# The SBUF pools of a two-layer hybrid decoder are created in another order

## The chip, the cores and the metric

The kernel runs on one core of a Trainium2 chip. The metric is device time in microseconds (us) for one execution. Engines are named as in the profile: PE is the matmul engine (TensorE), PEld its weight loads, DVE the vector engine, ACT the scalar engine, POOL the GpSimd engine, SP the engine that issues most DMAs. L365 is line 365 of the kernel.

## The reference

Two layers act on 256 tokens of width 1024, in float32:

```
h += 0.5 * SwiGLU_1(RMSNorm(h))                       # width 2816
u  = RMSNorm(h);  P = u @ W_in                        # one combined projection
y  = retention, Mamba-2 SSD, latent attention, differential attention   (256 x 512 each)
h += W_out( sum_i sigmoid(gate_i(u)) * (y_i @ W_branch_i) )
h += CrossAttention(RMSNorm(h), RMSNorm(mem))         # 4 heads, 256 memory rows
h += 0.5 * SwiGLU_2(RMSNorm(h))
```

and a last RMSNorm. Almost all of the arithmetic is in products of the 256 tokens with weight matrices.

## The kernel before

**Weights.** They are streamed from HBM in the order of use, in tiles of up to [128, 2048] float32 (1 MB). `fetch` issues one DMA on SP's queue into a tile `wr` (L327), then splits it in two float32r parts whose sum it is: ACT copies it, rounded, into `wh` (L334), and DVE writes the difference into `wl` (L335), each in two halves. There are three buffers each of `wr`, `wh` and `wl`. One tile is made ready ahead of the one that the matmuls use.

**Activations.** They are transposed on PE and split in the same way into high and low parts: `xh`, `xl` for the normed stream (pool `xp`, four tiles of 4 KB in each partition), and 4 KB tiles of pool `mp` (eleven buffers) for everything else: `hid` (the SwiGLU's hidden values), `yr`, `ym`, `yl`, `yd` (the four mixers), `xo0`, `xo1` (cross attention), `mm` (the memory). Smaller work tiles are in `fp` and `sp`, constants and `h` in `cp`.

**Products.** Each is three matmuls of parts: high times high, low times high, high times low. There are two loops that do nearly all of them.

```python
    def linear(kt, n, xT, evacs):          # L351; the matmul is L365
        ...
                for b in range(NB):
                    begin()
                    for part, w in ((0, hi), (1, hi), (0, lo)):
                        for k in range(m):
                            ...
                            pe.matmul(p_[b][:, :n], lhsT=xT(part, k0 + k)[:, b * P:(b + 1) * P],
                                      rhs=w[:, k * n:(k + 1) * n], start=first, stop=last)

    def linear_t(xT, evac):                # L371; the matmul is L383
        ...
                            o = k * 512 + (i * 2 + j) * P
                            pe.matmul(ps[i][:, j * 256:(j + 1) * 256], lhsT=ws[w][:, o:o + P], rhs=xT(part, k0 + k),
```

`lhsT` is the stationary operand (loaded by PEld, 128 columns) and `rhs` the moving one. In `linear` the activations are stationary and 512 columns of weights move; in `linear_t` 128 columns of weights are stationary and the 256 tokens move. PE's instructions keep the order in which they are written; the other engines' order is set by the tile framework, which also adds the waits. Chains of smaller steps (softmax, convolution, transposes) are put between the matmuls by hand.

**Pools.** `program` opens eight SBUF pools (L156 to L163). The framework puts them one behind the other in the order in which they are opened, from byte 16512 of each partition up, and the tiles of a pool likewise. All tiles that L365 and L383 read start at a whole number of 512 bytes from the start of their pool (4096 or 8192 bytes for a tile, 512, 1024 or 2048 for a slice in it); the one exception is the 424-column projection, whose slices are 1696 bytes apart.

Of the kernel before, what the change touches and what calls it, by code (L numbers as in the profile page):

```python
# [16 lines left out]
PSUM = bass.MemoryType.PSUM  # L17
# [13 lines left out]
BUCKETS = 32  # L31
# tiles of weights that are made ready before the matmuls that are traced
AHEAD = 1

# columns of w_in by use
_sizes = (256, 256, 512, 512, 512, 1024, 8, 256, 128, 32, 512, 512, 512, 4096)
_at = np.concatenate([[0], np.cumsum(_sizes)])
(O_RQ, O_RK, O_RV, O_RG, O_Z, O_XBC, O_DT, O_CQ, O_CKV, O_KR, O_DQ, O_DK, O_DV, O_GL) = (int(v) for v in _at[:-1])
# groups of 512 columns, in the order in which they are streamed
G_QK, G_RV, G_RG, G_X0, G_X1, G_Z, G_DQ, G_DK, G_DV, G_GL = range(10)  # L40
_groups = [O_RQ, O_RV, O_RG, O_XBC, O_XBC + 512, O_Z, O_DQ, O_DK, O_DV] + [O_GL + 512 * i for i in range(8)]
MISC = 256 + 128 + 32 + 8

# per-partition parameters of one layer: (name, columns)
_pcols = [("ffn1", 8), ("mix", 8), ("xa", 8), ("mem", 8), ("ffn2", 8), ("ssm", 4), ("qn", 2), ("kvn", 1), ("dn", 1),
          ("cw", 32), ("cb", 8)]
# parameters that every partition needs, of one layer
_bcols = [("dtb", 8), ("alog", 8), ("dsk", 8), ("lam", 256)]
# [11 lines left out]
BO, NBC = _offsets(_bcols)  # L60
# constants that depend on shapes alone
CO, NCC = _offsets([("ident", 128), ("tri", 384), ("dmask", 256), ("inv", 48), ("sel", 8), ("dec", 4 * 256)])
# [37 lines left out]
def lay(x, mem, positions, **w):  # L100
    """The program's inputs: the arrays given, laid out; and constants."""
    a = {k: np.asarray(v) for k, v in w.items()}
# [45 lines left out]
def program(tc, a, out, upto="all"):  # L148
# [4 lines left out]
    def sb(name, bufs):  # L153
        return ctx.enter_context(tc.tile_pool(name=name, bufs=bufs))

    cp = sb("cp", 1)  # L156
    wr = sb("wr", 3)
    wh = sb("wh", 3)
    wl = sb("wl", 3)
    xp = sb("xp", 1)  # L160
    fp = sb("fp", 2)
    sp = sb("sp", 4)
    mp = sb("mp", 11)  # L163
    lin = ctx.enter_context(tc.tile_pool(name="lin", bufs=4, space=PSUM))
# [23 lines left out]

    # ---- inputs that stay
    h = [[cp.tile([P, 512], F32, tag=f"h{b}{c}", name=f"h{b}{c}") for c in range(2)] for b in range(NB)]  # L190
# [31 lines left out]

    # ---- the order of work: linears one after another, and chains of smaller steps between them.
    # A chain yields how many half tiles of weights it lets pass, or what has to have happened before it goes on.
    chains = []
# [37 lines left out]

    # ---- weights, fetched in the order of use
    def chunks(srcs, kt, n):
# [43 lines left out]
    todo = list(plan())  # L309
    # a recent instruction of VectorE, for what is to be spread over the linears  # L310
    paced = None
    fetched = []
    # the last of the instructions that split weights, for what is to be queued behind it
    last = None

    def fetch(first=False):
        """The next tile of weights, as two float32r parts whose sum they are. The first one comes in pieces."""
        nonlocal last
        if not todo:
            return  # L320
        src, n = todo.pop(0)
        r = wr.tile([P, 2048], F32, tag="wr", name="wr")
        hi = wh.tile([P, 2048], F32R, tag="wh", name="wh")
        lo = wl.tile([P, 2048], F32R, tag="wl", name="wl")
        pieces = 4 if first else 2
        if not first:
            nc.sync.dma_start(r[:, :n], src)  # L327
        for i in range(pieces):
            s = slice(i * n // pieces, (i + 1) * n // pieces)
            if first:  # L330
                if i == 2:
                    nc.sync.dma_start(h[1][0], a["x"][1, :, :512])
                nc.sync.dma_start(r[:, s], src[:, s])
            last = act.activation(hi[:, s], r[:, s], AF.Copy)  # L334
            dve.tensor_tensor(lo[:, s], r[:, s], hi[:, s].bitcast(F32), ALU.subtract)  # L335
        fetched.append((hi, lo, n))
# [7 lines left out]

    # ---- building blocks
    def split(hi, lo, src):
        """hi + lo = src, in float32r; src is in SBUF or PSUM."""
        act.activation(hi, src, AF.Copy)
        dve.tensor_tensor(lo, src, hi.bitcast(F32), ALU.subtract)

    def linear(kt, n, xT, evacs):  # L351
        """Rows of tokens times weights [kt * 128, n], one or more; evac(b, psum) takes a block of rows."""
        ps = [[lin.tile([P, 512], F32, tag="lin", name="lin") for _ in range(NB)] for _ in evacs]
# [17 lines left out]
    def linear_t(xT, evac):  # L371
        """Weights [1024, 512] transposed times tokens: evac(i, psum) takes 256 columns as [128, 2, 256]."""
        ps = [lin.tile([P, 512], F32, tag="lin", name="lin") for _ in range(2)]
        for k0 in (0, 4):
            ws = weights(2048)
            for i in range(2):
                begin()
                for j in range(2):
                    for part, w in ((0, 0), (1, 0), (0, 1)):
                        for k in range(4):  # L380
                            o = k * 512 + (i * 2 + j) * P
                            # a start clears the flags of the whole bank: one for both halves
                            pe.matmul(ps[i][:, j * 256:(j + 1) * 256], lhsT=ws[w][:, o:o + P], rhs=xT(part, k0 + k),  # L383
# [6 lines left out]
    def transpose4(src, n=4):  # L390
        """Blocks of 128 columns of src, transposed, in one bank: [128, n, 128]."""
        ps = bank("tr")
# [4 lines left out]
    def split_gain(hi, lo, ps, gain, n=4):  # L397
        """hi + lo = a PSUM tile [128, n, 128] times a gain for each partition and n."""
        t = f2("sgt")[:, :n * P].rearrange("p (k t) -> p k t", k=n)
# [6 lines left out]
    def rstd_of(ss, n, m, name):  # L406
        """(ss / n + eps) ** -0.5 of m columns."""
        t = small("rs" + name, m)
# [9 lines left out]
    class Transposed:  # L418
        """src(b, c): [tokens, 512] for two blocks of columns, transposed and split; with a gain for each column.
        Each half starts as its columns are there."""  # L420

# [41 lines left out]
    def rows_of(r, name):  # L463
        """A value for each token, [P, NB], as rows [P, 256] alike on every partition."""
        ps = bank("rowp")
# [56 lines left out]

    # ---- tables that both layers share
    def tables():
# [19 lines left out]
        for b in range(NB):  # L544
# [18 lines left out]
            yield 2  # L563
        # lambda of the differential attention: -lambda for each layer
        for l in range(L):
# [9 lines left out]
            dve.tensor_scalar(nlam[:, l:l + 1], nlam[:, l:l + 1], li, None, ALU.subtract)  # L575
        # relative bias, times 8, with the causal mask: [queries, head, (block 0, keys 0) (block 1, keys 0 and 1)]
        rel = relt[:, :384]
# [9 lines left out]
        for i, t in enumerate(_thresholds()):  # L587
            yield 3
            # not around the change of stage
            while 60 <= now < 72:  # L590
# [8 lines left out]
    def rope(dst, src, tb, n_heads, hf):  # L599
        """dst = src rotated, [P, heads, 2 * hf]; tb: [cos, sin, -sin] of hf columns each."""  # L600
        s = src.rearrange("p h (e d) -> p h e d", e=2)
# [12 lines left out]
    def attend(b, scores, masks, scale, sbt):  # L614
        """Softmax numerators of a block of queries, in sbt [P, n, 256]; the sums' reciprocals. scores: PSUM for each."""
        n, nk = len(scores), (b + 1) * P
# [10 lines left out]
    def probs_t(pT, b, probs):  # L627
        """Transposed probabilities of a block of queries; pT: keys 0 [P, 4, 256] and keys 1 [P, 4, 128]."""
        for kb in range(b + 1):
# [5 lines left out]
    def mixers(l, xT, nxt):  # L635
# [10 lines left out]

        # -- retention
        qk = [f2("qk") for _ in range(NB)]
# [61 lines left out]

        # -- MLA's low ranks, and Mamba's steps
        dtx = small("dtx", 16).rearrange("p (b h) -> p b h", b=2)
# [23 lines left out]
        def mamba():  # L736
            yield ["misc"]
            x = dtx.rearrange("p b h -> p (b h)")
            e, z1, z2, p_ = (small(n, 16) for n in ("sp0", "sp1", "sp2", "sp3"))
            # softplus(x) = max(x, 0) + 2 artanh(e / (2 + e)) with e = exp(-|x|)  # L740
            dve.scalar_tensor_tensor(e, x, -1.0, x, ALU.mult, ALU.min)
# [24 lines left out]
            dve.tensor_copy(gc, pg[:, :16])  # L766
            # the running sums in two parts, for each block of tokens
            gr = sp.tile([P, NB, 16], F32R, tag="gr", name="gr", bufs=1)
# [3 lines left out]
            yield ["x0", "x1"]  # L772
            # xs on tokens
            xdt, xD = two("xdt"), two("xD")
# [65 lines left out]

        # -- Mamba-2: convolution, on channels
        for j in range(2):
# [19 lines left out]

        # -- gates and merge
        mg = []
# [30 lines left out]

        # -- MLA
        qT, kT, v = heads("mqT"), heads("mkT"), two("mv")
# [68 lines left out]

        # -- differential attention
        def on_rows(dst, name):
# [75 lines left out]

    # ---- memory, normalized, transposed and split
    def memory(l, mem, before):
# [187 lines left out]
```

## Time and profile before

| | |
|---|---|
| median of 3 runs | 1603.26 us (1602.47 to 1603.28) |
| span of the profiled execution | 1601.6 us |
| lies around the span | about 1.7 us (median less span) |
| PE busy | 1587.3 us (99%) |
| DVE busy | 1070.4 us (67%) |
| ACT busy | 825.2 us (52%) |
| mean DMA share, rate | about half, 176 GB/s |

The span runs from the first to the last instruction of one profiled execution. PE's busy time is the union of its matmuls' records, whose ends are modelled, so a busy PE does not say how closely the matmuls follow each other: that is read from the distance between their starts.

### The profile page before, as it was taken

The page shows a single profiled execution, that of the slowest core. Times are in us where ns is not written, and L with a number is a line of the kernel's source. Part 1 is how long each engine was busy: PE and PEld are TensorE (multiplying, and loading weights), DVE is VectorE, ACT ScalarE, POOL GpSimd, SP SyncE. Part 2 cuts the span into 40 slices and gives each one's busy share as a digit, 9 for nine tenths or more (in the row PEclk, how much of TensorE's full clock was granted, in tenths as well). Part 3 has the DMA queues.
Part 4 walks back from the last instruction along what each step waited for, and adds up shares of the span by engine and source line. Part 5 has one row for each costly group of instructions (what it writes and reads, how often), then busy time and mean ns, then how long its engine had stood idle before and what let it go on. Part 6 is the DMA issues. An engine that isn't in the chain of part 4 may idle for free.

```text
span 1601.6 us, 20813 instructions
## 1 busy us (share of the span) xinstructions
PE 1587.3 (99%) x8236; PEld 1349.4 (84%) x8236; DVE 1070.4 (67%) x1698; ACT 825.2 (52%) x1221; POOL 27.0 (2%) x39
## 2 busy tenths in 40 slices
PE   8999999999999999999999999999999999999998
PEld 6888889898888988888888888898988899888886
DVE  6787699998777666554465546697656766565543
ACT  6544446656655545444454444475575554454432
POOL 0000000000000000000000000000000000000000
PEclk9999999999999999999999999999999999999999
DMA  7555554454555544555555556444545554455541
GB/s 288 200 178 187 185 175 159 151 169 147 204 184 169 181 155 162 184 184 175 186 192 185 183 174 207 149 158 152 184 150 206 184 183 163 155 177 180 195 171 66
DMA packets 41713, 281.58 MB, mean 176 GB/s; under 512 B 4624, under 2 KB 5008, under 8 KB 9488
## 3 DMA queue, kind: packets, MB, share of 16 engines
q1 hardware_dynamic: 39600, 275.07, 50.2%
q10 hardware_dynamic: 2016, 5.19, 1.0%
q8 instruction: 64, 1.05, 0.3%
q14 instruction: 33, 0.27, 0.0%
HBM read 279.20 MB, written 1.05 MB: 175 GB/s over the span
## 4 chain that ended last, share of the span: by engine, by line
PE 98%; ACT 0%; DMA 0%; issue 0%; DVE 0%; SPq 0%; POOLq 0%; POOL 0%
PE lin L365 78%; PE lin L383 11%; PE tr L394 2%; PE ht L500 1%; PE xs L1094 1%; PE xo L1140 1%; PE up L905 1%; PE my L821 0%; PE ds L990 0%; DMA h<-x 0%; PE ms L941 0%; PE pt L632 0%; ACT wh L334 0%; PE my L823 0%; PE do L1013 0%
## 5 line engine op out<-in xcount | busy, mean ns | idle before, releaser
L335 DVE TENSOR_TENSOR wl<-wr,wh 128x1024 fp32r<-128x1024 f32 (+2 forms) x534 | 624.9, 1195 | 388.1 <-ACT wh L334 385.6
L334 ACT ACTIVATE wh<-wr 128x1024 fp32r<-128x1024 f32 (+2 forms) x534 | 533.4, 1033 | 518.5 <-PE lin L365 398.7
L365 PE MATMUL lin<-wh,xh 128*128 128x512 f32 (+1 forms) x1216 | 334.0, 396 | 0.2 <-ACT wh L334 0.2
L365 PE MATMUL lin<-wh,xl 128*128 128x512 f32 (+1 forms) x1216 | 325.9, 390 | 0.0
L365 PE MATMUL lin<-wl,xh 128*128 128x512 f32 (+1 forms) x1216 | 325.1, 389 | 0.0
L365 PEld LDWEIGHTS lin<-wh,xl 128*128 128x128 f32 x1216 | 228.8, 188 | 48.1
L365 PEld LDWEIGHTS lin<-wl,xh 128*128 128x128 f32 x1216 | 228.8, 188 | 47.7
L365 PEld LDWEIGHTS lin<-wh,xh 128*128 128x128 f32 x1216 | 222.5, 189 | 43.6 <-ACT wh L334 1.2
L365 PE MATMUL lin<-wh,hid 128*128 128x512 f32 x704 | 180.4, 396 | 0.0
L365 PEld LDWEIGHTS lin<-wh,hid 128*128 128x128 f32 x704 | 131.6, 188 | 31.4
L365 PE MATMUL lin<-wl,hid 128*128 128x512 f32 x352 | 97.7, 395 | 0.0
L365 PEld LDWEIGHTS lin<-wl,hid 128*128 128x128 f32 x352 | 66.1, 188 | 16.0
L510 ACT ACTIVATE sg<-lin,rffn 128x256 f32<-128x256 f32 x88 | 40.9, 464 | 65.2 <-PE lin L365 65.1
L596 DVE SCALAR_TENSOR_TENSOR bias<-relt,d,bias 128x384 f32<-128x384 f32 x124 | 69.8, 612 | 0.8
L383 PE MATMUL lin<-xh,wh 128*128 128x256 f32 x384 | 63.2, 287 | 0.0
L383 PE MATMUL lin<-xh,wl 128*128 128x256 f32 x384 | 61.7, 283 | 0.0
L383 PE MATMUL lin<-xl,wh 128*128 128x256 f32 x384 | 61.7, 283 | 0.0
L511 DVE SCALAR_TENSOR_TENSOR toks<-lin,rffn,sg 128x256 f32<-128x256 f32 x88 | 42.3, 481 | 25.7 <-ACT sg L510 25.7
L383 PEld LDWEIGHTS lin<-xh,wh 128*128 128x128 f32 x384 | 53.1, 191 | 0.3
L383 PEld LDWEIGHTS lin<-xh,wl 128*128 128x128 f32 x384 | 53.0, 192 | 0.0
L383 PEld LDWEIGHTS lin<-xl,wh 128*128 128x128 f32 x384 | 52.9, 191 | 0.0
L416 ACT ACTIVATE junk<-h 128x512 bf16<-128x512 f32 x36 | 22.4, 621 | 31.2 <-DVE h L484 17.2
(385 smaller groups left out, 1536.7 us busy)
## 6 DMA issues: line engine op xcount, KB each, us to landing
wr<-gu SPq DMA_DIRECT2D x87, 1024.0 KB, 5.0
wr<-win SPq DMA_DIRECT2D x68, 1024.0 KB, 5.0
wr<-dn SPq DMA_DIRECT2D x40, 1024.0 KB, 4.8
wr<-wbr SPq DMA_DIRECT2D x16, 1024.0 KB, 4.9
wr<-w_out SPq DMA_DIRECT2D x8, 1024.0 KB, 4.9
wr<-xa_wk SPq DMA_DIRECT2D x8, 1024.0 KB, 5.0
wr<-xa_wq SPq DMA_DIRECT2D x8, 1024.0 KB, 4.9
wr<-xa_wv SPq DMA_DIRECT2D x8, 1024.0 KB, 4.9
```

Of the source, the lines that this page charges most:

```text
L334: last = act.activation(hi[:, s], r[:, s], AF.Copy)
L335: dve.tensor_tensor(lo[:, s], r[:, s], hi[:, s].bitcast(F32), ALU.subtract)
L365: pe.matmul(p_[b][:, :n], lhsT=xT(part, k0 + k)[:, b * P:(b + 1) * P], rhs=w[:, k * n:(k + 1) * n], start=first, stop=last)
L383: pe.matmul(ps[i][:, j * 256:(j + 1) * 256], lhsT=ws[w][:, o:o + P], rhs=xT(part, k0 + k), start=k0 + k + part + w + j == 0, stop=k0 + k = ...
L394: pe.transpose(ps[:, k * P:(k + 1) * P], src[:, k * P:(k + 1) * P], ident)
L416: act.activation(j[:, :src.free_size()], src, AF.Square, accum_out=out_)
L500: pe.transpose(ps[:, k, blk(b)], toks[:, b, k * P:(k + 1) * P], ident)
L510: act.activation(sg, ps[:, :256], AF.Silu, scale=xT.r[:, b:b + 1])
L511: paced = dve.scalar_tensor_tensor(toks[:, b], ps[:, 256:], xT.r[:, b:b + 1], sg, ALU.mult, ALU.mult)
L596: dve.scalar_tensor_tensor(bias[:, hd], ge, d8[:, hd, i + 1:i + 2], bias[:, hd], ALU.mult, ALU.add)
L905: pe.matmul(ps[:, :n], lhsT=lowT[p_][:, k0 + k, blk(b)], rhs=wm[w][:, o + k * n:o + (k + 1) * n], start=i == 0, stop=i == len(seq) - 1)
L1094: pe.matmul(ps[:, j], lhsT=q[part][:, 2 * j + k, blk(b)], rhs=kT[c][w][:, 2 * j + k], start=not part + w + k, stop=w + k == 2)
```

## The change

The eight pools are opened in another order. Names, sizes and numbers of buffers stay, and so does all code behind them; comments were dropped, which moves line numbers by one or so (L365 becomes L366, L383 becomes L384).

```diff
+    xp = sb("xp", 1)
+    mp = sb("mp", 11)
+    fp = sb("fp", 2)
     cp = sb("cp", 1)
+    sp = sb("sp", 4)
     wr = sb("wr", 3)
     wh = sb("wh", 3)
     wl = sb("wl", 3)
-    xp = sb("xp", 1)
-    fp = sb("fp", 2)
-    sp = sb("sp", 4)
-    mp = sb("mp", 11)
```

No instruction moves: on every engine the queue of the changed program has the same instructions, operands by name and waits, row for row (2040 rows of PE, 1240 of DVE, 706 of ACT, 37 of POOL, 61 of SP when like neighbours are put together). What moves are the addresses. The built programs have the pools at these bytes of each partition, and the last two columns are the remainders by 256 (those by 128 are in brackets):

| pool | holds | before | after | start mod 256 before | after |
|---|---|---|---|---|---|
| wr | raw weights | 42976 to 67552 | 155424 to 180000 | 224 (96) | 32 (32) |
| wh | high part of weights | 67552 to 92128 | 180000 to 204576 | 224 (96) | 32 (32) |
| wl | low part of weights | 92128 to 116704 | 204576 to 229152 | 224 (96) | 32 (32) |
| xp | xh, xl | 116704 to 133088 | 16512 to 32896 | 224 (96) | 128 (0) |
| mp | hid, mm, yr ... xo1 | 184096 to 229152 | 32896 to 77952 | 32 (32) | 128 (0) |
| fp | work tiles | 133088 to 173024 | 77952 to 117888 | 224 (96) | 128 (0) |
| cp | h, constants | 16512 to 42976 | 117888 to 144352 | 128 (0) | 128 (0) |

## Rows read from the trace of the kernel before

**Rows 1.** The page: busy time (share of the span), number of instructions.

```profile
PE 1587.3 (99%) x8236; PEld 1349.4 (84%) x8236; DVE 1070.4 (67%) x1698; ACT 825.2 (52%) x1221; POOL 27.0 (2%) x39
...
PEclk9999999999999999999999999999999999999999
```

**Rows 2.** The page: the chain that ended last, by engine and by line.

```profile
PE 98%; ACT 0%; DMA 0%; issue 0%; DVE 0%; SPq 0%; POOLq 0%; POOL 0%
PE lin L365 78%; PE lin L383 11%; PE tr L394 2%; PE ht L500 1%; PE xs L1094 1%; PE xo L1140 1%; PE up L905 1%; PE my L821 0%; PE ds L990 0%; DMA h<-x 0%; PE ms L941 0%; PE pt L632 0%; ACT wh L334 0%; PE my L823 0%; PE do L1013 0%
```

**Rows 3.** Line L365 on PE: count, duration ns min/median/max, first and last start.

```profile
L365 PE MATMUL lin<-wh,xh x1216: 349/389/775, 8.4 to 1530.0; 128*128 128x512 f32 x168, 128*128 128x424 f32 x6
L365 PE MATMUL lin<-wh,xl x1216: 349/389/628, 10.3 to 1530.9; 128*128 128x512 f32 x168, 128*128 128x424 f32 x6
L365 PE MATMUL lin<-wl,xh x1216: 353/389/628, 12.0 to 1531.8; 128*128 128x512 f32 x168, 128*128 128x424 f32 x6
L365 PE MATMUL lin<-wh,hid x704: 392/394/483, 136.8 to 1593.4; 128*128 128x512 f32 x176
L365 PE MATMUL lin<-wl,hid x352: 390/394/403, 138.6 to 1593.8; 128*128 128x512 f32 x176
L365 PE MATMUL lin<-wh,mmh x64: 394/394/478, 559.4 to 1378.4; 128*128 128x512 f32 x64
...
L365 PE MATMUL lin<-wh,yrl x32: 393/394/398, 317.5 to 1119.2; 128*128 128x512 f32 x32
```

**Rows 4.** The same for line L383.

```profile
L383 PE MATMUL lin<-xh,wh x384: 277/283/470, 249.9 to 1349.5; 128*128 128x256 f32 x192
...
L383 PE MATMUL lin<-mmh,wh x128: 276/276/367, 509.5 to 1323.3; 128*128 128x256 f32 x128
```

**Rows 5.** The chain in order of time: start us, us, engine and line, matmuls.

```profile
1281.72 16.34 PE lin L365 x72
...
1305.40 19.05 PE lin L383 x168
...
1324.90 17.27 PE lin L383 x144
...
1538.24 56.01 PE lin L365 x240
```

**Rows 6.** The time line of PE where those pieces begin: start us, us, tiles.

```profile
1281.47 1.17 PE L365 MATMUL lin<-wh,xh 128*128 128x512 f32 x4
...
1305.16 0.71 PE L383 MATMUL lin<-mmh,wh 128*128 128x256 f32 x4
...
1324.66 0.71 PE L383 MATMUL lin<-xh,wh 128*128 128x256 f32 x4
...
1538.00 2.11 PE L365 MATMUL lin<-wh,hid 128*128 128x512 f32 x8
```

**Rows 7.** Whole span, PE, one line each: us, busy (instructions), clock, DMA.

```profile
0.00:1601.60 1601.60, 1282.09 (x5472) 1.00 0.51 176
...
0.00:1601.60 1601.60, 187.48 (x1536) 1.00 0.51 176
```

**Rows 8.** What PE, SP's queue and ACT waited for: us in total, times, longest.

```profile
PE lin L365 <- ACT wh L334: 0.2, 1, 0.2
...
SPq L327 <- DVE wl L335: 1301.1, 238, 14.9
...
ACT wh L334 <- PE lin L365: 398.7, 175, 4.5
```

**Rows 9.** Groups by line and form: the two splits; busy us, mean ns | idle before.

```profile
L335 DVE TENSOR_TENSOR wl<-wr,wh 128x1024 fp32r<-128x1024 f32 x502 | 600.2, 1220 | 368.0 <-ACT wh L334 367.3
L334 ACT ACTIVATE wh<-wr 128x1024 fp32r<-128x1024 f32 x502 | 511.5, 1053 | 484.5 <-PE lin L365 371.0 <-issue 85.3 <-PE lin L383 22.6
```

**Rows 10.** DMA issues: count, KB each, us from issue to landing.

```profile
wr<-gu SPq DMA_DIRECT2D x87, 1024.0 KB, 5.0
```

## The prediction

> **What bounds the kernel now.** I read the page first: PE is busy for 99% of the span, at a granted clock of 0.9 or more in every slice [rows 1]. Next the chain that ended last: 98% of it is PE, 78% the matmuls of `linear` (L365) and 11% those of `linear_t` (L383) [rows 2]. The waits say that this is no hidden wait for data: PE waited for a split weight once, for 0.2 us, while ACT waited 398.7 us for PE to give back `wh` buffers, and SP's queue 1301.1 us for `wr` buffers [rows 8]. So the time is the number of matmuls times the distance between their starts, and only that distance, or a new wait, can change it.
>
> Then I asked how large that distance is, and whether it is the same everywhere. It isn't. In the chain in order of time, 72 matmuls of L365 take 16.34 us, which is 226.9 ns each; 240 others of the same line take 56.01 us, 233.4 ns each [rows 5]. The time line shows what differs: the first piece has `xh` as its stationary operand, the second `hid` [rows 6]. For L383 the 144 matmuls with `xh` moving take 17.27 us, 119.9 ns each, and the 168 with `mm` moving 19.05 us, 113.4 ns each [rows 5, 6]. The durations of all of them repeat this: the median is 389 ns with `xh` or `xl` and 394 with every tile of `mp` on L365 (`yr` and `mm` as well as `hid`), and 283 against 276 on L383 [rows 3, 4]. The instructions of each pair have the same shape and type and the same weights' buffers. What differs is the pool in which the activation lies, so it is the address. That is what this change changes.
>
> **How much of the distance can depend on it.** [...] Each matmul then pays beside its columns 226.9 - 214.0 = 12.9 ns (L365, `xh`), 19.4 ns (L365, `hid`), 12.9 ns (L383, `xh`) or 6.4 ns (L383, `mm`). These are 2, 3, 2 and 1 times the same step, 6.5 ns or about 16 columns.
>
> **The change part by part.** No instruction is added, removed or moved, so the whole of the change is in the addresses. Before, weights and `xp` start at 96 bytes past a multiple of 128, `mp` at 32. After, weights start at 32, and `xp` and `mp` at 0. I take the step as the sum of a part for the moving and a part for the stationary operand. L383 gives the first: an activation that moves from 32 is one step (6.5 ns) cheaper than one that moves from 96. L365 gives the second: a stationary operand at 32 is one step dearer than one at 96. Position 0 is in no row. Its bounds are the two positions that are seen on either side of it, 32 bytes away each; I take the cheaper one for both operands, since a tile that starts at 0 lies in whole stretches of 128 bytes. The terms are:
>
> - L365, weights that move go from 96 to 32: 5472 matmuls [rows 7] x 6.5 ns = 35.6 us less. This is a position that was seen, if for another pool.
> - L365, `mp` tiles that are stationary go from 32 to 0. There are 5472 - 3 x 1216 = 1824 of them [rows 3, 7]; at the price of 96 that is 6.5 ns each, 11.9 us less; at the price of 32 nothing.
> - L365, `xh` and `xl` that are stationary go from 96 to 0: 3648 matmuls; nothing at the price of 96, 23.7 us more at that of 32.
> - L383, `xh` and `xl` that move go from 96 to 0: 1536 matmuls of the line [rows 7] less those of `mm` (three pairs of 128, one of which stands in [rows 4]) leave 1152; 7.5 us less at the price of 32, nothing at that of 96. `mm` (384) stays cheap, or loses 2.5 us.
> - L383, weights that are stationary go from 96 to 32: 1536 [rows 7] x 6.5 = 10.0 us more.
> - The other matmuls (some 10% of the chain, mostly transposes and the attention's small products) I leave at nothing: 1228 instructions at one step each would be 8 us at most, and their signs are mixed.
>
> The sum is -35.6 - 11.9 - 7.5 + 10.0 = -45.0 us. Against the profiled span that is 1601.6 - 45.0 = 1556.6 us; the median of the runs is 1.7 us above the span, so 1558 us.
>
> **What hides the rest, and what is late next.** ACT's and DVE's splits also read and write other addresses, and may take longer or shorter. They cost nothing as long as a tile is split faster than it is used: a full tile feeds 24 matmuls, 5.4 us at 226.9 ns and 5.3 us at 220.4, while ACT needs 2 x 1.053 us and DVE 2 x 1.220 us for it [rows 9]. The DMA lands 5.0 us after its issue [rows 10], with three buffers to fill. With the gain PE asks for weights 3% faster, 181 GB/s in place of 176; if the splits were to take twice as long, DVE's 1070 us would become the bound, and no row hints at that.
>
> [...] The rows show an address effect of 6.5 ns on PE alone [rows 3, 5]. [...]
>
> **The rivals.**
>
> *No gain: position 0 is as dear as the dearer neighbour.* Then `xh` on L365 loses 23.7 us, `mp` wins nothing, `xh` and `mm` on L383 pay for 96: -35.6 + 23.7 + 2.5 + 10.0 = +0.6 us, and the time stays at 1603 or 1604 us. [...] For it: nothing in the rows prices 0. Against it: both operands would have to come out at their dear end. Chance 0.08.
>
> *Slower: the distance between the two operands counts, not each one's position.* The rows fit that just as well. Modulo 256, moving start less stationary start is 224 - 224 = 0 where two steps are paid (both lines), 224 - 32 = 192 for `hid` (three steps), 32 - 224 = 64 for `mm` (one step). After, L365 has 32 - 128 = 160, and L383 has 96. The nearest rows are 192 and 64: every L365 matmul would take the 233.4 ns of `hid`, which costs 3648 x 6.5 = 23.7 us, and `xh` on L383 would win 1152 x 6.5 = 7.5 us: +16.2 us, 1619 us. Drawn on as a line (one column for 4 bytes, half a step for 32) L365 pays another 3.3 ns x 5472 = 18 us and L383 wins 3.3 ns x 1536 = 5 us: +29 us, 1632 us. The place is the next weight load, which PEld reads while the matmul before it streams: if the two reads meet in the same part of the memory, their distance decides. It decides as soon as the distance between starts on L365 with `xh` is above 226.9 ns. Chance 0.25.
>
> *A larger gain.* If position 0 is a step better than either neighbour as stationary operand, L365 comes down to some 214 ns and 5472 x 6.5 = 35.6 us more are won: 1523 us. It needs a matmul with nothing beside its columns, which no row shows. Chance 0.09.
>
> *A smaller gain.* One of the two unknown prices is the dear one for some of the tiles, and 10 to 30 us are left of the 45: 1573 to 1593 us. Chance 0.16.
>
> **How the numbers follow.** The forecast itself (1535 to 1573 us, the sum with a quarter of it either way and a little for the small products) gets 0.42; with the larger gain and the smaller one the kernel is faster with 0.67. A measurement of this kernel tells a change from none at about 0.2%, 3.2 us: that leaves 0.08 for no change and 0.25 for slower. Cases of both signs hold much of the chance, so the range reaches from 1532 us (which leaves out most of the larger gain) to 1628 us (which holds the nearer value of the slower rival and leaves out the drawn-on line).
>
> **What would show it.** The median durations and the distance between starts of the four pairs are the test. Right: L365 near 220 ns for `xh` and for `hid` alike (medians equal, at or below 389 ns less 7), and L383 near 120 ns for both activations. The distance rival would show `xh` rise to the 394 ns of `hid` on L365 while L383 with `xh` falls to 276. Rows of PE that are the same as before to the nanosecond would mean that addresses do not matter. The prediction is also wrong if PE begins to wait for `wh` or `wl` by more than a few us, or if ACT's or DVE's split changes by so much that buffers come late.

## The result, and the profile after

The changed kernel takes 1629.7 us (median of 4 runs, 1629.11 to 1630.43), the kernel before 1602.87 us in the runs beside them: a ratio of 1.0167, 95% interval 1.0154 to 1.0179. It is slower by 27 us, where the forecast was 45 us faster (1558 us), and lies 1.7 us above the upper end of the predicted range (1532 to 1628 us). The slower rival, drawn on as a line, had named 1632 us.

The page of the changed kernel: span, and busy us (share of the span) with the number of instructions.

```profile
span 1627.7 us, 20813 instructions
...
PE 1613.9 (99%) x8236; PEld 1355.5 (83%) x8236; DVE 1070.8 (66%) x1698; ACT 825.5 (51%) x1221; POOL 27.0 (2%) x39
```

The instructions are the same in number. DVE and ACT are busy for as long as in [rows 1], to within 0.4 us, and PE for 26.6 us longer, which is the whole of it: the span grew by 26.1 us.

The two lines on PE, to hold against [rows 3, 4] (count, duration ns min/median/max, first and last start):

```profile
L366 PE MATMUL lin<-wh,xh x1216: 353/397/774, 7.9 to 1555.8; 128*128 128x512 f32 x168, 128*128 128x424 f32 x6
...
L366 PE MATMUL lin<-wh,hid x704: 391/397/481, 139.7 to 1619.4; 128*128 128x512 f32 x176
...
L384 PE MATMUL lin<-xh,wh x384: 277/281/469, 253.9 to 1371.7; 128*128 128x256 f32 x192
...
L384 PE MATMUL lin<-mmh,wh x128: 277/281/364, 517.2 to 1345.4; 128*128 128x256 f32 x128
```

What differed before is now equal. On L366 `xh` and `hid` both have a median of 397 ns, dearer than the dearer of the two before (394); on L384 both activations have 281, between the 276 and the 283 of before.

The chain in order of time gives the distance between starts, for the same four pieces as in [rows 5] (start us, us, matmuls):

```profile
1302.22 16.86 PE lin L366 x72
...
1326.50 20.15 PE lin L384 x168
...
1347.10 17.28 PE lin L384 x144
...
1564.08 56.23 PE lin L366 x240
```

That is 234.2 ns for `xh` (before 226.9), 119.9 for `mm` (before 113.4), 120.0 for `xh` on L384 (before 119.9) and 234.3 for `hid` (before 233.4). Over the whole span, the busy time of each line's matmuls (second figure), against [rows 7]:

```profile
0.00:1627.70 1627.70, 1306.16 (x5472) 1.00 0.51 173
...
0.00:1627.70 1627.70, 189.76 (x1536) 1.00 0.51 173
```

L366 took 24.1 us more and L384 2.3 us more. No wait was added: PE still waits once for `wh`, and the splits wait for PE a little longer than in [rows 8].

```profile
PE lin L366 <- ACT wh L335: 0.2, 1, 0.2
...
ACT wh L335 <- PE lin L366: 412.9, 176, 4.5
```

### The profile page after: what moved, and what is told of

Its sections match the earlier page's. It is cut to its first block, busy times and chain, and to the rows that moved or that the text cites. A ratio compares the mean times of both kernels' runs of the same rounds, so it can differ in the third digit from the quotient of the medians.

```text
span 1627.7 us, 20813 instructions
## 1 busy us (share of the span) xinstructions
PE 1613.9 (99%) x8236; PEld 1355.5 (83%) x8236; DVE 1070.8 (66%) x1698; ACT 825.5 (51%) x1221; POOL 27.0 (2%) x39
## 4 chain that ended last, share of the span: by engine, by line
PE 98%; ACT 0%; issue 0%; DMA 0%; DVE 0%; SPq 0%; POOLq 0%; POOL 0%
PE lin L366 78%; PE lin L384 11%; PE tr L395 2%; PE ht L501 1%; PE xo L1141 1%; PE xs L1095 1%; PE up L906 1%; PE my L822 0%; PE ds L991 0%; PE ms L942 0%; DMA h<-x 0%; PE pt L633 0%; ACT wh L335 0%; PE my L824 0%; PE do L1014 0%
## 5 line engine op out<-in xcount | busy, mean ns | idle before, releaser
L366 PE MATMUL lin<-wh,xh 128*128 128x512 f32 (+1 forms) x1216 | 340.4, 402 | 0.2 <-ACT wh L335 0.2
L366 PE MATMUL lin<-wh,xl 128*128 128x512 f32 (+1 forms) x1216 | 333.7, 396 | 0.0
L366 PE MATMUL lin<-wl,xh 128*128 128x512 f32 (+1 forms) x1216 | 333.3, 396 | 0.0
L366 PEld LDWEIGHTS lin<-wl,xh 128*128 128x128 f32 x1216 | 229.7, 189 | 54.7
L366 PEld LDWEIGHTS lin<-wh,xl 128*128 128x128 f32 x1216 | 229.5, 189 | 54.3
L366 PEld LDWEIGHTS lin<-wh,xh 128*128 128x128 f32 x1216 | 223.1, 189 | 49.3 <-ACT wh L335 1.2
L366 PE MATMUL lin<-wh,hid 128*128 128x512 f32 x704 | 181.1, 397 | 0.0
L366 PEld LDWEIGHTS lin<-wh,hid 128*128 128x128 f32 x704 | 132.1, 188 | 31.7
L366 PE MATMUL lin<-wl,hid 128*128 128x512 f32 x352 | 98.0, 396 | 0.0
L366 PEld LDWEIGHTS lin<-wl,hid 128*128 128x128 f32 x352 | 66.3, 188 | 16.2
L384 PE MATMUL lin<-xh,wh 128*128 128x256 f32 x384 | 63.0, 286 | 0.0
L384 PE MATMUL lin<-xh,wl 128*128 128x256 f32 x384 | 61.6, 282 | 0.0
L384 PE MATMUL lin<-xl,wh 128*128 128x256 f32 x384 | 61.5, 282 | 0.0
L384 PEld LDWEIGHTS lin<-xh,wh 128*128 128x128 f32 x384 | 52.9, 189 | 0.3
L384 PEld LDWEIGHTS lin<-xl,wh 128*128 128x128 f32 x384 | 52.8, 189 | 0.0
L384 PEld LDWEIGHTS lin<-xh,wl 128*128 128x128 f32 x384 | 52.6, 188 | 0.0
```

## The experiments

The theory after the result is that of the slower rival: what counts is the **distance**, moving start less stationary start, modulo 256 bytes. The theory that it has to beat is the forecast's own, a price for each operand's **position**. The distances of the tiles, before and after, are those worked out in that rival.

**Sixteen distances, nothing else running (e1_sweep).** A program of its own: one tile `mov`, one tile `sta`, and for each cell 96 matmuls whose slices step by 2048 and 1024 bytes, as on L366. The cells are named by a letter for their form (w, v, n) and one for the distance (a is 0, b is 32 and so on).

```python
    for pre, n, mo in (("w", 512, 0), ("v", 512, 8), ("n", 256, 0)):   # offsets in 4-byte words
        for i in range(16):
            ps = cell(f"{pre}{NAMES[i]}", n, mo, (mo - 8 * i) % 128)
```

> This kernel leaves out the whole decoder and only repeats matmuls: cells of 96 matmuls each, one after the other, no other engine at work. In cells wa to wp 512 columns move from byte 0 of a 512-byte stretch and the stationary operand starts 0, 32, ... 480 bytes below it (modulo 512); in va to vp the moving operand starts at byte 32, with the same sixteen distances; in na to np 256 columns move from byte 0. The distance theory: the ns per matmul depend on the distance alone, so va to vp repeat wa to wp within 1 ns, and distances 0, 64, 160 and 192 give what the kernels show: 226.9 (0), 233.4 (192), about 234.3 (160) on 512 columns, 113.4 or 117.8 (64), 119.9 (0) and about 119.9 (96) on 256. If the period is 256, cells 8 apart agree. The position theory (a price for each operand): the v cells are all one price away from the w cells, by up to 13 ns in the same direction. A third theory, that other engines' reads and writes cause it: all cells the same, near 214 to 220 ns.

The time line of that run, one row a cell (start us, us, tiles). The distance between starts of a cell is the next row's start less its own, over 96.

```profile
167.55 22.56 PE L45 MATMUL wh<-mov,sta 128*128 128x512 f32 x96
189.95 21.95 PE L45 MATMUL wi<-mov,sta 128*128 128x512 f32 x96
211.74 22.55 PE L45 MATMUL wj<-mov,sta 128*128 128x512 f32 x96
...
368.19 21.95 PE L45 MATMUL va<-mov,sta 128*128 128x512 f32 x96
389.99 22.55 PE L45 MATMUL vb<-mov,sta 128*128 128x512 f32 x96
412.38 22.14 PE L45 MATMUL vc<-mov,sta 128*128 128x512 f32 x96
434.36 22.56 PE L45 MATMUL vd<-mov,sta 128*128 128x512 f32 x96
456.76 22.55 PE L45 MATMUL ve<-mov,sta 128*128 128x512 f32 x96
479.16 22.65 PE L45 MATMUL vf<-mov,sta 128*128 128x512 f32 x96
501.64 22.56 PE L45 MATMUL vg<-mov,sta 128*128 128x512 f32 x96
524.04 22.56 PE L45 MATMUL vh<-mov,sta 128*128 128x512 f32 x96
546.44 21.95 PE L45 MATMUL vi<-mov,sta 128*128 128x512 f32 x96
```

Worked out in this way from these rows, and from the n cells' rows in the same manner (ns per matmul):

| distance, bytes | 0 | 32 | 64 | 96 | 128 | 160 | 192 | 224 |
|---|---|---|---|---|---|---|---|---|
| 512 columns (va to vh) | 227.1 | 233.2 | 229.0 | 233.3 | 233.3 | 234.2 | 233.3 | 233.3 |
| 256 columns (na to nh) | 120.0 | 116.7 | 117.8 | 120.0 | 118.6 | 117.3 | 117.8 | 118.2 |

The second eight repeat the first (wi: 21.79 us over 96, 227.0 ns, as va), so the period is 256 bytes, and cells with the moving operand at byte 0 and at byte 32 agree (to 0.1 ns: wb and vb 233.2, wf 234.3 and vf 234.2; wa has the start of the run in it). On 512 columns distance 160, where the change put L366, is the dearest of all, at the 234.2 ns that the kernel shows; 0, where `xh` had been, is the cheapest. On 256 columns the order is another: 0 and 96 are the dearest there. No other engine was at work beside the cells, and still their 227.1 and 234.2 ns are the kernels' paces (226.9 and 234.2), so it takes no other engine to bring them about. The distance theory stands, with one blemish: at 64 the sweep has 117.8 ns where the kernel before had 113.4. In the kernel before, the first 24 matmuls on `mm` also took 117.9 each, and only the 168 behind the next break 113.4 (the chain of the kernel before, in its first layer):

```profile
509.69 2.83 PE lin L383 x24
512.53 0.87 PE tr L394 x8
513.40 19.05 PE lin L383 x168
```

So this distance has two settled paces, 117.9 and 113.4 ns.

**All positions moved by 64 bytes, distances kept (e2_shift64).** In the kernel before:

```diff
+    pad = sb("pad", 1)
+    pad.tile([P, 16], F32, tag="pad", name="pad")
     cp = sb("cp", 1)
```

> The kernel before with an unused tile of 64 bytes ahead of all pools, so that every position moves by 64 and every distance stays. The distance theory: every line as before, 1603 us, with xh at 226.9 ns, hid at 233.4, mm at 113.4. The position theory of the prediction: hid (now at 96 by 128) becomes two steps cheaper and the weights that move (now at 32) one step cheaper, so L365 with hid near 220 ns, mm near 126 ns, and the kernel about 25 us faster.

1603.23 us against 1603.19, ratio 1.0 (0.999 to 1.0009). Its chain, `mm` and `hid`:

```profile
1303.89 19.05 PE lin L385 x168
...
1536.73 56.01 PE lin L367 x240
```

To the hundredth of a microsecond these are the rows of before [rows 5]. The position theory asked for 25 us here and falls.

**The `mp` tiles moved to distance 0 in the old order (e3_mp192), and all weights moved to distance 0 in the new order (e4_after96).** In the kernel before and in the kernel after:

```diff
+    pad = sb("pad", 1)
+    pad.tile([P, 48], F32, tag="pad", name="pad")
     mp = sb("mp", 11)
```

```diff
+    pad = sb("pad", 1)
+    pad.tile([P, 24], F32, tag="pad", name="pad")
     wr = sb("wr", 3)
```

> The kernel before with an unused tile of 192 bytes ahead of pool mp, which takes all its tiles to 224 modulo 256, as the weights and xh. The distance theory: L365 with hid, mm and the mixers falls from 233.4 to 226.9 ns (1824 matmuls, 11.9 us less), L384's counterpart with mm rises from 113.4 to 119.9 (384, 2.5 us more): 1593.5 us. The position theory of the prediction gives the same here. No effect of the distance: 1603 us.

> The kernel after the change with an unused tile of 96 bytes ahead of the weights' pools, which takes weights to 128 modulo 256, where the activations are: all distances 0, in the changed order of pools. The distance theory: all of L365's counterpart at 226.9 ns, L384's at 119.9, so 1593 to 1594 us as with the 192 bytes in the kernel before, 36 us faster than after the change. If the order of the pools (weights above activations) counts instead: the time stays near 1630 us.

e3 takes 1593.99 us, ratio to the kernel before 0.9941 (0.9926 to 0.9955); e4 takes 1593.06 us, 0.9933 (0.9918 to 0.9948). The chain of e3 and then that of e4, `mm` and `hid` each:

```profile
1297.32 20.16 PE lin L385 x168
...
1530.15 54.46 PE lin L367 x240
```

```profile
1295.72 20.15 PE lin L386 x168
...
1528.46 54.45 PE lin L368 x240
```

In both, `hid` comes to 226.9 ns (in e3 from 233.4, in e4 from 234.3) and `mm` is at 119.9 or 120.0. The new order of pools with 96 unused bytes is 36.6 us faster than without, and within 1 us of the old order at the same distances. So the order as such costs nothing that shows here; the distance of 160 bytes that it happened to leave on L366 costs these 36.6 us. These two are also faster than both kernels of the study.

**A distance that no kernel had (e6_after64).** The same edit with 16 words in place of 24, which leaves 224 on L366's counterpart and 32 on L384's.

> The kernel after the change with 64 unused bytes ahead of the weights' pools: L366 then has distance 224 and L384 32, which no tile of any kernel so far had. If the table of the first sweep holds in the full kernel, L366 takes 233.3 ns and L384 116.7 ns: against the kernel after, 5376 x 0.95 + 1536 x 3.2 = 10 us less, 1619 to 1620 us. If only distance 0 is special and all others are alike: 1629 to 1630 us.

1619.67 us, ratio to the kernel before 1.0102 (1.0085 to 1.0119): inside the microsecond that the table had named. `xh` on 256 columns, and `hid`:

```profile
1337.93 16.80 PE lin L386 x144
...
1553.57 56.01 PE lin L368 x240
```

116.7 and 233.4 ns, where the table has 116.7 and 233.3.

**Finer steps, and fewer stationary columns (e5_fine).** The same program with other cells:

```python
    for pre, m in (("h", 64), ("q", 32)):                    # stationary columns
        for i, d in enumerate((0, 32, 160)):
            cell(f"{pre}{NAMES[i]}", 512, 16, (16 - d // 4) % 64, m)
    for pre, n in (("w", 512), ("n", 256)):
        for i in range(17):                                  # -32 to 32 bytes in steps of 4
            ps = cell(f"{pre}{NAMES[i]}", n, 16, 16 - (i - 8))
```

> Only repeated matmuls again, 96 to a cell, the decoder left out. Cells ha, hb, hc (64 stationary columns) and qa, qb, qc (32) have distances 0, 32 and 160 with 512 moving columns. If the weight load's reads collide with the moving operand's, the time beside the columns shrinks with the number of stationary columns: 32, 48 and 50 columns' worth at 128 become about 16, 24 and 25 at 64 and 8 to 12 at 32, so 220 to 224 ns and 217 to 218 ns. If it is a fixed price of a switch between two matmuls, all six cells stay at 226.7 to 234.3 ns. Cells wa to wq (512 columns) and na to nq (256) take the distance from -32 to 32 bytes in steps of 4: if the memory is read in lines of 32 bytes or more, steps inside one line cost the same as its ends or lie between them (226.7 to 233.3 ns; 116.7 to 120 ns); a best value between 0 and 32 bytes on both forms would point to a better placement than distance 0.

```profile
34.12 22.33 PE L45 MATMUL hb<-mov,sta 128*64 128x512 f32 x96
56.29 21.93 PE L45 MATMUL hc<-mov,sta 128*64 128x512 f32 x96
78.06 22.40 PE L45 MATMUL qa<-mov,sta 128*32 128x512 f32 x96
100.29 22.56 PE L45 MATMUL qb<-mov,sta 128*32 128x512 f32 x96
...
301.04 22.48 PE L45 MATMUL wh<-mov,sta 128*128 128x512 f32 x96
323.35 21.93 PE L45 MATMUL wi<-mov,sta 128*128 128x512 f32 x96
345.12 21.93 PE L45 MATMUL wj<-mov,sta 128*128 128x512 f32 x96
366.89 22.56 PE L45 MATMUL wk<-mov,sta 128*128 128x512 f32 x96
389.28 22.56 PE L45 MATMUL wl<-mov,sta 128*128 128x512 f32 x96
```

The collision in proportion fails. The cells hb to qc stay between 226.8 and 233.3 ns, in the bounds of the other expectation, a price for each matmul; the first, ha, has the start of the run in it (254.4 ns over its 96 matmuls) so that its mean is no pace to hold against them. It is no single price, though: with 64 stationary columns distances 32 and 160 take 230.9 and 226.8 ns, with 32 columns distances 0, 32 and 160 take 231.6, 233.3 and 230.6. A quarter of the load does not cost a quarter, and the cheap distance moves: with 32 columns it is 160. In steps of 4 bytes, 512 columns take 232.4 ns at -4 bytes (wh), 226.8 at 0 and at 4 (wi, wj) and 233.2 at 8 (wk); no distance is below 226.7. Between 8 and 32 bytes the price goes down and up again (228.3 ns at 16, 233.3 at 32). With 256 columns the lowest is 115.5 ns at -8 bytes (ng, 11.09 us over 96) and the highest 121.8 at -24 (nc), both outside the 116.7 to 120 ns that were expected. So lines of 32 bytes or more, as I had supposed them, are not borne out.

**Which operand is met, and at what width (e7_mech).** Positions alternate between even and odd matmuls, or the stationary operand is one column 128 times over, or the width or the type changes:

```python
    cell("both", 512, (0, 0), (0, 0))           # own 0, next 0
    cell("none", 512, (0, 0), (24, 24))         # own 160, next 160
    cell("own", 512, (0, 40), (0, 40))          # own 0, next 96 and 160
    cell("next", 512, (0, 40), (40, 0))         # own 96 and 160, next 0
    cell("bca", 512, (0, 0), (0, 0), broadcast=True)
    ...
    cell("halfz", 512, (0, 0), (0, 0), bmov, bsta)      # bfloat16, distance 0
    cell("halfx", 512, (0, 0), (48, 48), bmov, bsta)    # bfloat16, distance 160
```

> Only repeated matmuls, 96 to a cell, the decoder left out. Which pair of operands counts: in cell own each matmul has distance 0 to its own stationary operand and 96 or 160 to the next matmul's; in cell next it is the other way round; both and none are the controls (0 and 160 to both). If the next matmul's weight load, which runs while this one streams, is what meets it: next is at 226.7 ns as both, own near 233 to 234 as none. If the own operand counts: the reverse. Cells bca and bcb read one stationary column again and again (128 times the same word): if the load's walk over the same lines is the cause, both come out alike and below 226.7. Cells midz and midx (384 columns), smallz and smallx (128): a price for each matmul stays at 13 to 21 ns beside the columns' 160 and 53; a price for each column shrinks with them. Cells halfz and halfx do it in bfloat16, with half the bytes for each column: if the bytes that are read are the limit, both lie near 214 to 216 ns and the distance is worth nothing.

```profile
34.52 21.92 PE L51 MATMUL both<-mov,sta 128*128 128x512 f32 x96
56.28 22.65 PE L51 MATMUL none<-mov,sta 128*128 128x512 f32 x96
78.77 22.62 PE L51 MATMUL own<-mov,sta 128*128 128x512 f32 x96
101.23 22.24 PE L51 MATMUL next<-mov,sta 128*128 128x512 f32 x96
123.30 22.40 PE L51 MATMUL bca<-mov,sta 128*128 128x512 f32 x96
145.54 22.40 PE L51 MATMUL bcb<-mov,sta 128*128 128x512 f32 x96
167.79 16.82 PE L51 MATMUL midz<-mov,sta 128*128 128x384 f32 x96
184.44 16.81 PE L51 MATMUL midx<-mov,sta 128*128 128x384 f32 x96
201.09 10.83 PE L51 MATMUL smallz<-mov,sta 128*128 128x128 f32 x96
211.76 10.88 PE L51 MATMUL smallx<-mov,sta 128*128 128x128 f32 x96
222.48 20.89 PE L51 MATMUL halfz<-bmov,bsta 128*128 128x512 bf16 x96
243.21 20.88 PE L51 MATMUL halfx<-bmov,bsta 128*128 128x512 bf16 x96
```

both takes 226.7 ns, none 234.3, own 234.0 and next 229.9. Distance 0 to the own stationary operand alone is worth next to nothing (0.3 ns); to the next one alone it is worth some 60% of the gain (4.4 of 7.6 ns). The next one is loaded while the matmul streams; in the kernel before, four loads on L365 and their four matmuls are (start us, us):

```profile
1282.25 0.87 PEld L365 LDWEIGHTS lin<-wh,xl 128*128 128x128 f32 x4
1282.48 1.07 PE L365 MATMUL lin<-wh,xl 128*128 128x512 f32 x4
```

The loads begin 0.23 us, about one matmul, ahead. That points to the load beside the stream, though not to it alone: what the alternation of positions costs by itself is in no cell.

With a single column read 128 times, the distances 0 and 160 take the same, 231.7 and 231.8 ns (bca, bcb): alike, as expected, but not below 226.7. With this load the distance is worth 0.1 ns (7.6 between both and none), and yet a matmul takes 5 ns more than in both. So which words the load reads bears on the difference between distances, and is not all that takes the time.

At 384 columns the two distances took the same (16.82 and 16.81 us a cell, 173.4 ns a matmul), so the table can't be carried to a width that was not measured. At 128 columns they took 111.1 and 111.7 ns. The price for each matmul that was expected, 13 to 21 ns beside the columns, holds at 384 (13 ns beside 160) and fails at 128 (58 ns beside 53). What the columns take is here an estimate from the rows of before: 107.0 ns for 256 of them (226.9 less 119.9), 0.418 ns each. In bfloat16 the distance is worth nothing (20.89 and 20.88 us a cell) and a matmul takes 215.9 ns (halfz), 11 less than the best in float32r and 2 above the columns' 214.0: most of the price is gone in a type that brings half the bytes for each column. That it is the bytes, and not something else about the type, is not shown.

## Why the prediction was wrong

- **What bounds the kernel** was right: the distance between the starts on PE, with no wait behind it. All of the 26 us is there.
- **That the address decides it** was right too, and the 6.5 ns between `xh` and `hid` came out of rows that e2 and e3 confirm. The 214.0 ns that the prices are counted from are twice the 107.0 between L365 and L383 with `xh` (226.9 less 119.9 [rows 5]), my estimate of what 512 columns take. As a step of which every price is a multiple it does not hold: the sweep has 229.0 and 234.2 ns, neither a whole number of steps above 226.9. The result is an effect of the addresses alone.
- **The step that failed** is "I take the step as the sum of a part for the moving and a part for the stationary operand". Positions have no price: moving everything by 64 bytes changed nothing (e2, 1603.23 against 1603.19 us), and in the sweep cells with the moving operand at 0 and at 32 agree to 0.1 ns. Three rows, at distances 0, 192 and 64, fitted both readings equally well, and I gave the wrong one the greater chance. The largest term, 35.6 us for weights that go "from 96 to 32", therefore does not exist: those matmuls took 7.3 ns more (`xh`) or 0.9 ns more (`hid`). The whole miss lies on L365, where the terms came to 47.5 us less and 24.1 us more were measured.
- **What came true by luck.** On L383 the position terms came to +2.5 us, with both activations near 120 ns, and 2.3 us and 119.9 and 120.0 ns were measured. But the two prices that cancel there for `xh` do not exist (e2). That `xh` and `hid` would be equal on L365 came true as well, at 234 ns in place of 220.
- **The rival** of the distance had the right variable and sign and, drawn on as a line, nearly the time: 1632 against 1629.7 us. Its parts were less good. It had 236.7 ns for L365 at 160, measured 234.3, and a gain on L383, where `mm` lost 6.5 ns a matmul and `xh` kept its pace. That the sum comes so near is partly luck: it had some 42 us more on L365 and 12 us less on L383, against 24.1 and 2.3 us more, so two errors cancel. Between the rows that were known the dependence is no line but the table above. Its account of the place, two reads that meet, is only partly borne out (4.4 of 7.6 ns in e7), fails in its proportions (e5), and no run shows the reads themselves.
- **"An address effect of 6.5 ns on PE alone"** was right as far as the runs go: the paces with nothing else running are those of the kernel (227.1 and 234.2 ns in e1, 226.9 and 234.2 there). For float32r with 512 columns the effect comes to 226.7 against 234.3 ns (e7, distances 0 and 160). The runs do not say what it is that meets, or where.
- **What lies beside the path** was right: the splits are no slower, and no buffer came late.

In sum for the change: the 26.4 us of the two lines' busy time. From the pace, 3552 matmuls of 512 columns with `xh` at 7.3 ns give 25.9 us, 1824 with `mp` tiles at 0.9 ns give 1.6 us and 384 with `mm` at 6.5 ns give 2.5 us, 30 us. Summed over the starts in the two traces, `xh` on L366 took only 22.4 us more, the `mp` tiles 1.5 and `mm` on L384 2.3. The excess is there because before, matmuls with `xh` took a few to fall into the cheap pace after each break, so that part of them did not have it to lose: the first four after a break average 255.8 ns in both traces, the next four differ by 4.5 ns, and from the fourth four on it is 7.4 (by fours, the first sixteen of one stretch took 1.01, 0.92, 0.92 and 0.90 us; after the change one took 1.01 and then 0.94). What stays open is why, on 512 columns, one distance in 256 bytes settles into a cheaper pace and what sets the others.

## What to carry to other kernels

In this kernel, where PE is the bound and its matmuls are float32r with 512 or 256 columns, the order of pools was also a choice of the distance between the tiles that move and those that are loaded, and it cost 3% of each matmul with `xh` on 512 columns (226.9 to 234.2 ns) without a single instruction or wait added. In a kernel like it, compare the distance between starts of matmuls of one shape across their tiles; if it differs, put a few unused bytes ahead of a pool and measure: here 96 bytes gave 36.6 us back. When rows fit two laws, spend the first run on a shift that keeps one law's variable and changes the other's.

## What the runs showed of the hardware that was not expected

- The pace went by the distance modulo 256 bytes (e1, 512 columns: 227.0 ns at 256 as 227.1 at 0, 233.2 at 32 and at 288), and a step of 4 bytes counted: 232.4 ns at -4 bytes, 226.8 at 0 and at 4, 233.2 at 8, on 512 columns (e5).
- The settled pace at distance 0 repeats: 54.45 us for 240 matmuls in e4, 54.46 in e3. Other distances settled at other paces (229.0 ns at 64, 234.2 at 160, e1), and one at two: `mm` in the kernel before took 117.9 ns ahead of a break and 113.4 behind it.
- Fewer stationary columns did not make a float32r matmul cheaper at distance 0: 231.6 ns with 32 columns against 226.7 with 128. At distance 160 they did, but not in proportion: 226.8 with 64 and 230.6 with 32 against 234.3 with 128.
- bfloat16 with the same shape takes 215.9 ns (halfz), and 0 and 160 are alike (20.89 and 20.88 us a cell). No float32r cell of 512 columns comes nearer to it than some 11 ns (226.7, both).
